# A two-layer decoder trunk: pairs by seven products, transposes in eights, a normalization finished after the product, and a table of places

## The chip, the cores and the metric

The kernel runs on one core of a Trainium2 chip. The metric is the device time of one execution in microseconds (us). Three runs of the kernel before took 1648.97, 1651.66 and 1651.95 us; their median is 1651.66 us.

## The reference

Tokens: 512 rows of 1024 features. The trunk has two layers, each with a half-weighted SwiGLU feed-forward (FFN), a token mixer and a second FFN; layer 0 mixes with a gated linear recurrence (RG-LRU), layer 1 with a causal spatial gate over chunks of 128 positions. So there are four FFNs, called f1 to f4 here, in the order f1, recurrence, f2, f3, spatial gate, f4.

```python
def rms_norm(x, g):
    y = xf * lax.rsqrt(jnp.mean(xf * xf, axis=-1, keepdims=True) + NORM_EPS)
    return y * g
def swiglu(x, w_in, w_out):                     # w_in 1024 x 5632, w_out 2816 x 1024
    g, u = jnp.split(x @ w_in, 2, axis=-1)
    return (jax.nn.silu(g) * u) @ w_out
def recurrent_mixer(x, ...):                    # w_in 1024 x 2048
    y, r = jnp.split(x @ w_in, 2, axis=-1)
    r = causal_depthwise_conv(r, conv_w, conv_b)
    h = rg_lru(r, ...)                          # two block-diagonal gates, then a scan over the rows
    return (jax.nn.gelu(y) * h) @ w_out
h = x
for i in range(2):
    h = h + 0.5 * swiglu(rms_norm(h, ffn1_norm[i]), ...)
    h = h + mixer(rms_norm(h, mix_norm[i]), ...)
    h = h + 0.5 * swiglu(rms_norm(h, ffn2_norm[i]), ...)
return rms_norm(h, final_norm)
```

## The kernel before, in words

**Arithmetic.** Every operand of a matrix product is cut into a rounded part ("hi") and the rest ("lo"); a product is three matmuls, hi by hi, lo by hi, hi by lo. The hi part is an ACT copy (L96), the lo part a DVE subtraction (L87); `split` does it for activations, `Sub.split` for a weight block of 128 x 1024 numbers (tiles `raw`, `whi`, `wlo`).

**Seven products.** `seven` computes a 2 x 2 block product with seven products instead of eight: P1, P2, P5, P6, P3, P7, Q4, each in one or more cuts of the inner dimension. P1, P6, P7 and Q4 gather in the PSUM banks A, P2 in B, P5 and P3 in C; in the output products Q4 has its own bank Q. The left sides are blocks of the activations (A11, A12, A22; the names give token half and feature half) and sums of them (S1 from A21, S2, S4, S3, in that order). The right sides are sums of weight blocks, made by DVE additions or by adding DMAs from POOL. After its last cut a product is read out (`p1` to `q4`): products that share a bank must not start before the readout of the one ahead.

**FFN.** An FFN has 22 column tiles of 128: in three parts, a pair of two tiles and a chunk of four, then twice two chunks of four. `chunk` uses `seven`; `pair_plain` (L695) computes the two tiles with eight products of 512 columns, gate and value side by side, and is the first work of each FFN. After each part `out_blocks` multiplies with `w_out` and adds to the residual `X`. Between them the hidden blocks are transposed on PE (128 x 128 each, tile `e`), four blocks after one product and four after the next, into a pool of two PSUM banks (`aux`).

**Norms.** RMSNorm's factor is applied after the product, by row, except ahead of the recurrence: there the product comes out with the rows along the free axis, so `TileNorm` (L490) scales the rows of `X` first (tile `xn`), transposes them (`xt`, L516) and cuts them into `zh`, `zl`; the first 256 rows are done when the first half of the residual is done, the other 256 when the last product (Q4) of f1 is.

**Order.** The program is a list `subs` of product cuts. The loop at the end goes through it: at step `i` it runs the actions hooked to the phases "pre" and "mid", with the weight splits up to three steps ahead (`SPLIT_AHEAD`) between them, then "rest", the loads, the matmuls of step `i`, then "end" and "late". Engines run their own instructions strictly in this order of issue, so the place of an action says what it stands behind on its engine. The places are written at each call of `hook`. Loads are issued by SP, adding DMAs by POOL.

Of the kernel before, what the change touches and what calls it, by code (L numbers as in the profile page):

```python
# [11 lines left out]
ALU = mybir.AluOpType  # L12
# [17 lines left out]
FF_PARTS = (("p", 4), (4, 4), (4, 4))  # L30
# [6 lines left out]
KORDER = (0, 2, 4, 6, 1, 3, 5, 7)  # L37
# [15 lines left out]
def trunk(ctx: ExitStack, tc: tile.TileContext, a: dict, out: bass.AP):  # L53
# [158 lines left out]

    def run(phase):
        for fn in hooks.pop((now[0], phase), []):
            fn()
# [17 lines left out]
    class S:  # L233
        z = None
        rt = None

# [4 lines left out]
    class Group:  # L241
# [12 lines left out]
        def turn(self, src, where=None):  # L254

            ps = (where or aux)("e")[:, : self.n * H]
            for q in range(self.n):
                for s in range(2):
                    o = q * H + s * P
                    nc.tensor.transpose(ps[:, o : o + P], src(q, s), ident)  # L260
            return ps
# [19 lines left out]
        def stage(self, n, name, src, gains=None, parts=True, where=None):  # L281

            st = {}
            hook(n, "end", lambda: st.update(ps=self.turn(src, where)))
            first = name == "A21"
            hook(n + 1, "pre" if first else "mid", lambda: self.take(name, st.pop("ps"), gains))
            if parts:
                hook(n + 1, "mid", lambda: self.parts("S1" if first else name))

        def both(self, n, name, src, then, then_src):  # L290

            st = {}

            def take():
                self.take(name, st.pop(name))
                self.take(then, st.pop(then))
                for b in (name, then):
                    if b != "A22":
                        self.parts("S1" if b == "A21" else b)

            hook(n, "end", lambda: st.update({name: self.turn(src), then: self.turn(then_src)}))
            hook(n + 1, "mid", take)
# [29 lines left out]
    def seven(block, cuts, left, w, posts, order=None, own=False, apart=False, joined=None):  # L332
# [6 lines left out]
        bk, raw, held = {}, {}, []  # L339
# [4 lines left out]
        def mm_of(prod, ci):  # L344
# [5 lines left out]
            def mm(sub):  # L350
# [6 lines left out]
                for s in range(2):  # L357
                    ps = bk[name, s]
# [10 lines left out]
                    if closes and prod in posts:  # L369
                        posts[prod](s, ps)  # L370
            return mm

        for prod, ci in order:
# [5 lines left out]
            if prod == "P1":  # L379
                r = raw[11, ci] = new(0, 0)  # L380
            elif prod == "P2":
                r = new(1, 0)
            elif prod == "P5":
                if own:
                    raw[11, ci] = new(0, 0, (0, 1))
                    if joined:
                        then = block(1, 1, cuts[ci])
                else:
# [3 lines left out]
            elif prod == "P6" and joined:  # L392
                r, then = raw[11, ci], block(1, 0, cuts[ci])
# [5 lines left out]
            elif prod == "P7":  # L399
                r = new(0, 1, (1, 1)) if own else raw[12, ci]  # L400
            else:
                r = raw[11, ci]
# [6 lines left out]

    def square(t, n):  # L410
        junk = slot(name="junk")
        act(junk, xt(t, n), AF.Square, accum_out=ss[:, n * TT + t : n * TT + t + 1])

    class Root:
# [7 lines left out]
        def root(self):  # L422
            act(self.s, self.v, AF.Sqrt)

        def get(self, r):
            q = tiny(self.w)
# [6 lines left out]
    def rstd(n, *phases, cols=slice(0, TT), new=True):  # L433
# [3 lines left out]
        def mean():  # L437
            st["r"] = Root((ss[:, :TT][:, cols], ss[:, TT:][:, cols]), cols.stop - cols.start)

        def newton():  # L440
            if new:
                S.rt = cp.tile([P, TT], F32, tag="rt", name=nm("rt"))
            st["r"].get(S.rt[:, cols])

        for (d, phase), fn in zip(phases, (mean, lambda: st["r"].root(), newton)):
            hook(n + d, phase, fn)
# [3 lines left out]
    def squares(n, phase, name):  # L450
        t0, c = QUARTER[name]
        hook(n, phase, lambda: (square(t0, c), square(t0 + 1, c)))

    class BlockNorm:


        def __init__(self, grow, block=False):
            self.g = [Group(2), Group(2)]
            self.grow, self.block = grow, block
# [5 lines left out]

        def quarter(self, name):
            n = now[0]
            squares(n + 1, "mid", name)
# [953 lines left out]
```

## Time and profile before

| | us |
|---|---|
| median of three runs | 1651.66 |
| the profiled execution | 1650.1 |
| its span on the core | 1648.3 |
| PE busy in the span | 1619.0 (98%) |
| DVE busy | 1379.7 (84%) |
| ACT busy | 1043.5 (63%) |
| POOL busy | 220.2 (13%) |

The profiled execution is 1.6 us under the median, and its span 1.8 us under its own time. PE's busy time counts from the start of a matmul to its modelled end, and matmuls overlap: what a matmul costs in a stream is the distance from start to start, not its duration. The mean granted clock of PE is 0.996 of full speed over the span.

### The profile page before, as it was taken

Reading aid. Unit: us, or ns where it says so; the run is one execution under the profiler, and the core shown is the slowest. Engines: PE = TensorE matmul, PEld = TensorE weight load, DVE = VectorE, ACT = ScalarE, POOL = GpSimd, SP = SyncE. Lnnn points to the kernel's source line nnn. Section 1 sums busy time; section 2 is a strip of 40 time slices with the busy share of each in tenths; the row PEclk is TensorE's granted clock in tenths of the full one; section 3 lists DMA queues with packets and bytes.
Section 4 is the critical chain, followed back from the end, with each engine's and each line's share of the span. In section 5 each row is a group of like instructions: output and inputs, shape, how many; then the busy total and the mean of one; then the engine's idle time right before and its main releaser. Section 6 shows DMA issues by size and latency. Waiting matters only on the chain. (4 is left out here: it accounts for less than half of the span.)

```text
span 1648.3 us, 20809 instructions
## 1 busy us (share of the span) xinstructions
PE 1619.0 (98%) x7451; PEld 1330.3 (81%) x7451; DVE 1379.7 (84%) x1824; ACT 1043.5 (63%) x1502; POOL 220.2 (13%) x199
## 2 busy tenths in 40 slices
PE   8999999989999999999999999999999999999997
PEld 6788888878878888888888888888887788888885
DVE  5998897877798897887988977878978988879777
ACT  6656656666857656556676565566885766565655
POOL 1111111100010111111102111111211011121120
PEclk9999999999999999999999999999999999999999
DMA  6767876952363876876838768768887557686693
GB/s 206 166 174 171 205 170 151 217 139 77 102 152 91 185 174 161 216 182 156 204 97 181 172 163 208 180 159 204 219 193 182 145 123 191 166 205 165 158 232 83
DMA packets 163463, 277.20 MB, mean 168 GB/s; under 512 B 11440, under 2 KB 37664, under 8 KB 163360
## 3 DMA queue, kind: packets, MB, share of 16 engines
q1 hardware_dynamic: 114400, 183.79, 35.9%
q0 software_dynamic: 47168, 90.25, 32.6%
q10 hardware_dynamic: 1792, 1.84, 0.4%
q8 instruction: 58, 0.95, 0.2%
q14 instruction: 45, 0.37, 0.1%
HBM read 273.74 MB, written 2.10 MB: 167 GB/s over the span
## 5 line engine op out<-in xcount | busy, mean ns | idle before, releaser
L96 ACT ACTIVATE whi<-raw 128x1024 fp32r<-128x1024 f32 (+1 forms) x545 | 562.4, 1034 | 412.2 <-PE A L367 112.6
L87 DVE TENSOR_TENSOR wlo<-raw,whi 128x1024 fp32r<-128x1024 f32 (+1 forms) x545 | 646.7, 1189 | 192.9 <-ACT whi L96 191.9
L366 PE MATMUL A<-whi,hi 128*128 128x512 f32 x1016 | 405.5, 399 | 3.3 <-DVE x L93 3.3
L367 PE MATMUL A<-whi,lo 128*128 128x512 f32 x1016 | 398.4, 392 | 3.2 <-DVE lo L87 3.1
L368 PE MATMUL A<-wlo,hi 128*128 128x512 f32 x1016 | 398.2, 392 | 0.3 <-DVE wlo L87 0.3
L367 PEld LDWEIGHTS A<-whi,lo 128*128 128x128 f32 x1016 | 191.7, 189 | 43.6 <-DVE lo L87 5.7
L368 PEld LDWEIGHTS A<-wlo,hi 128*128 128x128 f32 x1016 | 191.7, 189 | 41.9 <-DVE wlo L87 0.7
L366 PEld LDWEIGHTS A<-whi,hi 128*128 128x128 f32 x1016 | 191.8, 189 | 41.3 <-issue 3.7
L367 PE MATMUL C<-whi,lo 128*128 128x512 f32 x560 | 218.6, 390 | 1.2 <-DVE lo L87 1.0
L366 PE MATMUL C<-whi,hi 128*128 128x512 f32 x560 | 218.5, 390 | 0.0
L368 PE MATMUL C<-wlo,hi 128*128 128x512 f32 x560 | 218.0, 389 | 0.0
L136 POOL DMA_DIRECT2D raw<-in_ffn_w_in_dram x80 | 96.4, 1205 | 755.7 <-DVE raw L87 588.8
L87 DVE TENSOR_TENSOR raw<-raw,raw 128x1024 f32<-128x1024 f32 (+1 forms) x118 | 141.4, 1199 | 0.5
L136 POOL DMA_DIRECT2D raw<-in_ffn_w_out_dram x74 | 85.5, 1162 | 379.3 <-DVE wlo L87 145.9
L87 DVE TENSOR_TENSOR lo<-a,hi 128x512 fp32r<-128x512 f32 (+1 forms) x194 | 125.9, 657 | 10.5 <-ACT hi L96 10.1
L367 PEld LDWEIGHTS C<-whi,lo 128*128 128x128 f32 x560 | 105.1, 188 | 25.4 <-DVE lo L87 3.8
L366 PEld LDWEIGHTS C<-whi,hi 128*128 128x128 f32 x560 | 105.1, 188 | 22.1 <-ACT c L96 0.3
L368 PEld LDWEIGHTS C<-wlo,hi 128*128 128x128 f32 x560 | 105.1, 188 | 21.6
L96 ACT ACTIVATE hi<-a 128x512 fp32r<-128x512 f32 (+1 forms) x194 | 115.9, 600 | 4.6 <-DVE a L87 2.4
L96 ACT ACTIVATE c<-A 128x512 f32<-128x512 f32 x132 | 77.6, 595 | 59.1 <-PE A L368 58.6
L366 PE MATMUL B<-whi,hi 128*128 128x512 f32 x280 | 112.2, 401 | 0.0
L368 PE MATMUL B<-wlo,hi 128*128 128x512 f32 x280 | 109.3, 390 | 0.0
(160 smaller groups left out, 2093.8 us busy)
## 6 DMA issues: line engine op xcount, KB each, us to landing
raw<-in_ffn_w_in_dram SPq DMA_DIRECT2D x160, 512.0 KB, 4.4
raw<-in_ffn_w_out_dram SPq DMA_DIRECT2D x100, 512.0 KB, 5.3
raw<-in_ffn_w_in_dram POOLq DMA_DIRECT2D x80, 512.0 KB, 7.6
raw<-in_ffn_w_out_dram POOLq DMA_DIRECT2D x62, 512.0 KB, 8.3
raw<-in_sg_w_in_dram SPq DMA_DIRECT2D x20, 512.0 KB, 6.2
raw<-in_rec_w_in_dram SPq DMA_DIRECT2D x16, 512.0 KB, 3.9
raw<-in_ffn_w_in_dram SPq DMA_DIRECT2D x30, 256.0 KB, 4.0
raw<-in_sg_w_in_dram POOLq DMA_DIRECT2D x12, 512.0 KB, 8.5
```

The lines of the kernel that those rows point to most:

```text
L87: nc.vector.tensor_tensor(out=o, in0=x, in1=y, op=op)
L96: nc.scalar.activation(out=o, in_=x, func=f, **k)
L136: nc.gpsimd.dma_start(out=self.v, in_=src, accum_op=ALU.add)
L366: nc.tensor.matmul(ps, zh, wh, start=begin, stop=False, **k)
L367: nc.tensor.matmul(ps, zl, wh, start=False, stop=False, **k)
L368: nc.tensor.matmul(ps, zh, wl, start=False, stop=end, **k)
```

## The change

Six things change at once.

- **Pairs by seven products.** In f2, f3 and f4 the pair of column tiles goes through `chunk` and `seven` too, with 256 columns per product and all four inner blocks in one cut. f1 keeps `pair_plain`, in the middle of its first chunk (`between`). The chunk of four comes first in every FFN.
- **Transposes in eights.** The blocks of two products (A11 and A12, or A22 and A21) are transposed together, in `both` and `BlockNorm.turn`; a transposing bank comes from `aux` or from the matmul pool, by the table.
- **New opening.** f1 starts with P1 and P2 of the chunk. The loads alternate between a quarter of a row block of `x` and a weight block.
- **Last product's order.** f4's last output goes P1, P2, P6, P5, P7, Q4, P3 instead of P1, P5, P2, P6, P7, Q4, P3, with the weight sums rearranged to fit.
- **Half-wide norm.** `RecNorm` scales and transposes only the first 256 rows ahead of the recurrence's products. The other 256 are transposed unscaled, and their factor, laid along the free axis by two transposes (`rtw`), multiplies the right half of each of the sixteen product banks on DVE (`wide`).
- **The table.** `PLAN` has 916 entries: 201 weight splits one or two steps ahead instead of three, 121 banks for transposes, and the places of readouts and other actions; `soon` looks a place up, and readouts of `seven` may be put off.

```diff
+LATER_PARTS = ((4, 2), (4, 4), (4, 4))
+
+PLAN = {
+    "L0": 1, "L1": 2, "L10": 2, "L101": 1, "L104": 2, "L110": 2, "L111": 1, "L112": 2, "L114": 1, "L115": 1,
...
+    "f1c0postP3": (0, "late"), "f1c0postP5": (0, "end"), "f1c0s3": (4, "end"),
...
-KORDER = (0, 2, 4, 6, 1, 3, 5, 7)
+KORDER = (4, 5, 6, 7, 0, 1, 2, 3)
...
+    def soon(key, d, phase, fn, n=None):
+        d, phase = PLAN.get(key, (d, phase))
+        hook((now[0] if n is None else n) + d, phase, fn)
+
+    def home(key):
+        return bank if PLAN.get(key + "@") else aux
...
                     if closes and prod in posts:
-                        posts[prod](s, ps)
+                        when = PLAN.get(f"{key}post{prod}")
+                        if when is None:
+                            posts[prod](s, ps)
+                        else:
+                            late.add((name, s))
+                            hook(now[0] + when[0], when[1],
+                                 lambda s=s, ps=ps: (posts[prod](s, ps), late.remove((name, s))))
...
             if prod == "P1":
                 r = raw[11, ci] = new(0, 0)
+                if joined:
+                    then = block(0, 1, cuts[ci])
...
             elif prod == "P6" and joined:
-                r, then = raw[11, ci], block(1, 0, cuts[ci])
+                tile = raw[12, ci] = new(0, 1, (1, 1))
+                r, then = new(0, 0), block(1, 0, cuts[ci])
+                raw[6, ci] = r
...
+        def wide(self):
+            ps = self.ps["rt"] = aux("rt")
+            for t in range(2):
+                nc.tensor.transpose(ps[:, t * P : (t + 1) * P], S.rt[:, 2 + t : 3 + t].to_broadcast([P, P]), ident)
...
+            elif name == "A22":
+                soon("rnt1", 1, "end", lambda: self.turn("A22", self.plain))
+                soon("rnk1", 2, "mid", lambda: self.take("A22"))
...
-        ORDER = [(p, ci) for p in ("P1", "P5", "P2", "P6", "P7", "Q4", "P3") for ci in range(2)]
+        ORDER = [(p, ci) for p in ("P1", "P2", "P6", "P5", "P7", "Q4", "P3") for ci in range(2)]
...
+        def wide(ps):
+            tt(ps[:, H:], ps[:, H:], S.wide, ALU.mult)
...
     raws[0].halves = True
-    load_x(0, 512, 256)
-    load_x(0, 768, 256)
-    load_more(2)
-    load_x(0, 0)
+    for n, c in enumerate((0, 256, 512, 768)):
+        load_x(0, c, 256)
+        load_more(n + 1)
     load_x(2, 512)
+    load_more(5)
     load_x(2, 0)
     load_more()
...
-        upto = ahead.get(i, i + SPLIT_AHEAD)
-        for q in range(i, min(upto + 1, len(subs))):
-            if i >= 2 and q == upto and q + 1 < len(subs):
-                subs[q + 1].add()
-            subs[q].split()
+        for q in range(i, min(i + SPLIT_AHEAD + 1, len(subs))):
+            if q - PLAN.get(f"L{q}", SPLIT_AHEAD) <= i:
+                subs[q].split()
+            elif i >= 2:
+                subs[q].add()
```

Three places show how the order moves. First, PE in f4's last output, at the end of P6. Before, P7 follows at once in the same bank A:

```order
L368 MATMUL A_14065<-wlo_14154,hi_14183 128x512
L366 MATMUL A_14065<-whi_14153,hi_14183 128x512
L367 MATMUL A_14065<-whi_14153,lo_14184 128x512
L368 MATMUL A_14065<-wlo_14154,hi_14183 128x512
L366 MATMUL A_14064<-whi_14179,hi_14205 128x512
L367 MATMUL A_14064<-whi_14179,lo_14206 128x512
L368 MATMUL A_14064<-wlo_14180,hi_14205 128x512
L366 MATMUL A_14064<-whi_14179,hi_14205 128x512
```

Now P5 stands behind P6:

```order
L554 MATMUL A_14344<-whi_14391,hi_14443 128x512
L555 MATMUL A_14344<-whi_14391,lo_14444 128x512
L556 MATMUL A_14344<-wlo_14392,hi_14443 128x512
L554 MATMUL C_14496<-whi_14421,hi_14077 128x512
L555 MATMUL C_14496<-whi_14421,lo_14078 128x512
L556 MATMUL C_14496<-wlo_14422,hi_14077 128x512
```

The 24 matmuls of P5, in bank C, now lie between P6 and P7.

Second, PE at the start of the recurrence, after two half products of 24 matmuls (`r`). Before, the transposes of the other 256 rows read `xn`, which holds scaled rows:

```order
L218 MATMUL r_3262<-zh_3168,whi_3136 128x256
L219 MATMUL r_3262<-zl_3169,whi_3136 128x256
L220 MATMUL r_3262<-zh_3168,wlo_3137 128x256
L516 MATMUL xt_3287<-ident,xn_3223 128x128
L516 MATMUL xt_3287<-ident,xn_3227 128x128
```

Now, after one half product, they read `x` itself:

```order
L411 MATMUL r_3205<-zh_3179,whi_3083 128x256
L412 MATMUL r_3205<-zl_3180,whi_3083 128x256
L413 MATMUL r_3205<-zh_3179,wlo_3084 128x256
L730 MATMUL xt_3230<-ident,x 128x128 x4
L730 MATMUL xt_3235<-ident,x 128x128 x4
L411 MATMUL r_3256<-zh_3151,whi_3111 128x256
L412 MATMUL r_3256<-zl_3152,whi_3111 128x256
```

These eight need the third quarter of `X` (A22) alone; eight more follow one half product later.

Third, ACT in the recurrence, after the first five squares of the decay (`a<-g`). Before, a weight split, the last two gates (`g`, a table of their own) and a tanh stand ahead of the square roots (`tl<-tl`) on which the scans wait:

```order
L96 ACTIVATE a_811_3849<-g_3673 128x512
L96 ACTIVATE whi_3853<-raw_3410 128x1024
L96 ACT_TABLE_LOAD
L96 ACTIVATE g_3859<-gate_3824,vec 128x512
L96 ACTIVATE g_3861<-gate_3828,vec 128x512
L96 ACTIVATE tl_3863<-g_3859,lru_c 128x512
L96 ACT_TABLE_LOAD
L96 ACTIVATE tl_3496<-tl_3496 128x512
```

Now the square roots come first:

```order
L280 ACTIVATE a_807_3854<-g_3669 128x512
L280 ACT_TABLE_LOAD
L280 ACTIVATE tl_3489<-tl_3489 128x512
L280 ACTIVATE tl_3555<-tl_3555 128x512
L280 ACTIVATE tl_3608<-tl_3608 128x512
L280 ACTIVATE tl_3673<-tl_3673 128x512
L280 ACTIVATE tl_3714<-tl_3714 128x512
L280 ACTIVATE whi_3903<-raw_3457 128x1024
L280 ACTIVATE whi_3907<-raw_3459 128x1024
L280 ACT_TABLE_LOAD
L280 ACTIVATE g_3911<-gate_3832,vec 128x512
L280 ACTIVATE g_3913<-gate_3836,vec 128x512
```

The square roots have moved ahead of the last gates, and two weight splits have moved behind them.

514 lines of the change are left out of this document (297 added, 217 removed), and 175 rows, old and new, of the table PLAN.

## The prediction

> **What bounds the kernel now.** I read the page first, then a table of stages (busy time of each engine in stretches of the span), then PE's waits by releaser, and last the timeline at the places which these name.
>
> ```profile
> span 1648.3 us, 20809 instructions
> PE 1619.0 (98%) x7451; PEld 1330.3 (81%) x7451; DVE 1379.7 (84%) x1824; ACT 1043.5 (63%) x1502; POOL 220.2 (13%) x199
> ```
>
> PE is busy 98% of the span, so time can come from two sources only: less PE work, or less of PE's idle time. The stages show where that idle time is (start:end, length, then busy time and instructions by engine, the granted clock, DMA share and rate):
>
> ```profile
> core 0: us, PE busy (x) PEld busy (x) DVE busy (x) ACT busy (x) POOL busy (x), PEclk, DMA share, GB/s
> 0.00:40.00 40.00, 34.44 (x150) 24.98 (x150) 22.67 (x38) 26.18 (x49) 5.33 (x15) 1.00 0.64 212
> 40.00:110.00 70.00, 67.38 (x300) 53.73 (x301) 65.66 (x100) 45.26 (x69) 11.16 (x10) 1.00 0.76 174
> 320.00:353.00 33.00, 31.22 (x141) 24.41 (x139) 29.13 (x46) 21.48 (x37) 2.41 (x2) 1.00 0.66 154
> 353.00:367.00 14.00, 10.60 (x69) 9.93 (x69) 11.00 (x26) 9.52 (x22) 0.00 (x0) 0.88 0.28 81
> 367.00:460.00 93.00, 93.00 (x477) 79.70 (x476) 70.76 (x96) 69.18 (x100) 3.61 (x3) 1.00 0.33 94
> 460.00:480.00 20.00, 17.83 (x72) 14.33 (x71) 20.00 (x31) 9.77 (x13) 2.41 (x2) 0.91 0.56 120
> 480.00:1236.00 756.00, 755.40 (x3461) 622.26 (x3460) 642.27 (x802) 488.59 (x701) 107.52 (x91) 1.00 0.73 175
> 1236.00:1300.00 64.00, 61.48 (x310) 49.78 (x309) 55.73 (x92) 40.29 (x64) 7.25 (x6) 1.00 0.71 181
> 1600.00:1630.00 30.00, 26.68 (x113) 21.51 (x112) 24.19 (x33) 16.65 (x25) 3.61 (x3) 0.94 0.53 91
> ```
>
> Length less PE busy: 8.2 us in the first 110, 5.2 around the norm ahead of the recurrence (320 to 367), 2.2 at its end, 2.5 in the spatial mixer, 3.3 before the last products, and 0.6 in the 756 us of f2, f3 and their surroundings. Three of these stages have a lowered clock as well. At 0.88, 0.91 and 0.94 over 14, 20 and 30 us, 1.7 to 1.8 us go in each.
>
> ```profile
> PE A L366 <- DVE x L93: 3.3, 1, 3.3
> PE A L367 <- DVE lo L87: 3.1, 3, 2.2
> PE xt L516 <- ACT xn L96: 2.7, 3, 2.1
> PE e L260 <- DVE c L93: 2.1, 3, 1.0
> PE e L260 <- DMA x<-in_x_dram: 1.9, 2, 1.5
> PE warm L1308 <- DVE warm L1303: 1.3, 1, 1.3
> ```
>
> So the waits are few and long, each with an address: a readout in the last output, left sides after the scans, scaled rows ahead of the recurrence, hidden blocks, and `x` at the start. The clock follows the long ones:
>
> ```profile
> 462.79 0.80 PE L367 MATMUL A<-whi,lo 128*128 128x512 f32 x1 [2.17 <-DVE lo L87]
> 463.80 0.63 PE L366 MATMUL A<-whi,hi 128*128 128x512 f32 x1
> 464.23 0.63 PE L367 MATMUL A<-whi,lo 128*128 128x512 f32 x1
> 12.26 1.06 PE L260 MATMUL e<-ident,x 128*128 128x128 f32 x8 [1.54 <-DMA x<-in_x_dram]
> ```
>
> After 2.17 us of idle time the matmuls start 0.43 us apart; the idle 1.54 us of the opening lies in a stage at clock 1.00. "TensorE: Matmul & The Clock Gate" of the Trainium skill (section "Why this matters for your kernels") allows gaps up to about 3 us; here 2.17 us were enough, and the trace decides.
>
> **The change part by part.** *Pairs (f2, f3, f4).* What a matmul costs in a stream is the distance between starts. At 512 columns the rows below lie 26 matmuls apart, at 256 columns (the recurrence, both kinds of row) 17 and 18:
>
> ```profile
> 24.04 0.39 PE L717 MATMUL p<-whi,lo 128*128 128x512 f32 x1
> 29.93 0.39 PE L716 MATMUL p<-whi,hi 128*128 128x512 f32 x1
> 358.01 0.28 PE L219 MATMUL r<-zl,whi 128*128 128x256 f32 x1
> 360.05 0.28 PE L218 MATMUL r<-zh,whi 128*128 128x256 f32 x1
> 354.80 0.28 PE L218 MATMUL r<-zh,whi 128*128 128x256 f32 x1
> 357.15 0.28 PE L218 MATMUL r<-zh,whi 128*128 128x256 f32 x1
> ```
>
> That is 5.89 / 26 = 0.2265 us, then 2.04 / 17 = 0.120 and 2.35 / 18 = 0.131 us; half of 0.2265 would be 0.113. A pair took 8 products of 12 matmuls of 512: 96 x 0.2265 = 21.7 us. Now it is 7 products of 24 matmuls of 256: 168 x 0.120 = 20.2 us. Three pairs: **-4.8 us**, from -8.2 (0.113) to +0.6 (0.131). I take 0.120, the steady stretch; the slower one falls where DVE was cutting the same operands. By the Trainium skill, "TensorE: Matmul & The Clock Gate" (section "Back-to-back issue gap"), 256 columns would take 256 / 2.4 + 2.5 = 109 ns and the term would be an estimated -10.3 us, while its last section advises dimensions of at least 512; the rows show a price between, and they decide.
>
> On the other engines a pair costs one split more, and ten readouts of 256 columns instead of four:
>
> ```profile
> L96 ACT ACTIVATE whi<-raw 128x1024 fp32r<-128x1024 f32 (+1 forms) x545 | 562.4, 1034 | 412.2 <-PE A L367 112.6
> L87 DVE TENSOR_TENSOR wlo<-raw,whi 128x1024 fp32r<-128x1024 f32 (+1 forms) x545 | 646.7, 1189 | 192.9 <-ACT whi L96 191.9
> L87 DVE TENSOR_TENSOR s<-e,a 128x256 f32<-128x256 f32 x4 | 1.7, 413 | 0.0
> ```
>
> On DVE that is 1.2 + 6 x 0.41 = 3.7 us per pair. I cost it at nothing, because DVE is idle 114 us of the 756 between 480 and 1236; without that cover it would be 11 us for the three.
>
> *Last output.* PE waits 3.3 us for P6's readout from bank A before P7 may start, and a slow clock adds 1.8. In the new order 24 matmuls of P5, 24 x 0.2265 = 5.4 us, stand between them, more than wait and readout together. P3 is late next, if anything, and has P7 and Q4 ahead of it (10.9 us). **-5.1 us** (0 to -5.1).
>
> *Norm ahead of the recurrence.* 320 to 367 loses 5.2 idle and 1.7 in the clock. The second set of transposes waited for rows that need Q4's readout, squares, root and scaling. Now they need readouts alone, and Q4's has two half products, 2 x 24 x 0.120 = 5.8 us, and eight transposes as cover; the factor is needed only when the right half of the first bank is complete. The first set moves between the halves of Q4, which gives its rows 2.7 us more but its cutting 2.7 us less ahead of the first half product. I take **-6.0** of 6.9; the other bound, if the cutting is late by 1 us more than now, is +1. The price is sixteen multiplications on DVE at 0.41 = 6.6 us, and two transposes. DVE has 22 us free between 367 and 460.
>
> *End of the recurrence.* 2.2 idle and 1.8 in the clock. There the scans and not the products are late:
>
> ```profile
> 426.99 1.28 ACT L96 ACT_TABLE_LOAD   x1
> 431.47 2.71 ACT L96 ACTIVATE tl<-tl 128x512 f32<-128x512 f32 x5
> 432.13 0.69 DVE L87 TENSOR_TENSOR pr<-pr,tl 128x512 f32<-128x512 f32 x1 [2.71 <-ACT tl L96]
> ```
>
> From 432.13 on DVE works without a pause and the first left side lands at 462.8. With the square roots moved ahead of gates and a split, the table load follows at 426.99 - 1.03 = 425.96 and the first root at about 427.3 instead of 431.5; a multiplication ahead takes back 0.4, so the scans start 3.8 us sooner. By the order, one more weight split (1.2) and five multiplications (2.1) stand between first scan and left side, so it lands 0.5 us sooner. That leaves 1.7 us of idle time, between the 1.54 that left the clock alone and the 2.17 that did not. **-2.0 us**, from -4.0 (wait gone) to +3.3 (the head start is not used).
>
> *Opening and f1's first part.* 8.2 us idle, of which 1.3 (`warm`) stay. The waits for `x` go if each quarter comes with its weight block. Against it: by PE's order three transposed quarters, not two, now stand ahead of the first product, so 1.83 MB must land instead of 1.05; at 212 GB/s that is up to 3.7 us. Then 48 matmuls (10.9 us) run on data that have landed. I take **-4.0**, from -6.9 to +2.5.
>
> *Spatial mixer.* 2.5 us idle; its small products are spread out in eights between larger ones, which leaves DVE time for each: **-2.0** (-2.5 to 0). The single waits of the 756 us: **-0.3**.
>
> *Transposes in eights.* Their number stays (616 and 618 matmuls of 128 columns in the two programs); the runs fall from 144 to 84. A run of four and of eight, up to the second matmul behind it:
>
> ```profile
> 628.90 0.60 PE L260 MATMUL e<-ident,c 128*128 128x128 f32 x4
> 629.57 0.39 PE L367 MATMUL A<-whi,lo 128*128 128x512 f32 x1
> ...
> 1252.34 1.03 PE L260 MATMUL e<-ident,c 128*128 128x128 f32 x8
> 1253.44 0.40 PE L367 MATMUL A<-whi,lo 128*128 128x512 f32 x1
> ```
>
> Two fours take 2 x 0.67 - 0.23 = 1.11 us for the same matmuls, an eight 1.10: 60 x 0.01 = **-0.6** (0 to -1).
>
> *New waits.* The table moves 201 splits from three steps ahead to two or one, on ACT and DVE. Behind a split that waits for a free buffer stands all of ACT's other work (the 412 us of idle time ahead of `whi`, 112.6 of them waiting for PE), so this frees readouts. But a split takes 1.03 + 1.19 = 2.2 us and a step of 12 matmuls 2.7: one DVE instruction of 1.2 us ahead makes a split that is one step ahead 0.7 late, and PE waits for it. 76 are one step ahead. I allow three: **+2**, from 0 to +12.
>
> The sum: -4.8 - 5.1 - 6.0 - 2.0 - 4.0 - 2.0 - 0.3 - 0.6 + 2 = -22.8. From the profiled execution, 1650.1, that is a span of 1625.5 and a time of 1627.3; the median of the runs lies 1.6 above the profiled one, so I predict **1628.9 us**.
>
> **Rivals.** *Narrow matmuls bring nothing*: at 0.131 the pairs cost +0.6 instead of -4.8, so 1634. For it speaks that this distance stands in the trace and that DVE will be busier there; against it the longer steady stretch. The skill's advice on 512 columns is this rival.
>
> *Nearly all idle time goes*: every wait above except the warm-up is filled. Pairs -4.8, the stages -5.1 - 6.9 - 4.0 - 6.9 - 2.5 - 0.6, transposes -0.6: 1651.7 - 31.4 = 1620. For it: the waits are few and each gets work put in front. Against: DVE stays at 84% and more.
>
> *Splits too close* (slower than before): if more than 33 of the 76 splits that are one step ahead are 0.7 us late, the 22.8 + 2 us are eaten; with 60 late the time is 1651.7 - 24.8 + 42 = 1669. For it: DVE already waits 191.9 us for `whi`, so splits arrive barely ahead. Against: PE's waits for `wlo` are almost nothing now, and ACT has 37% free.
>
> *The table takes back what the rest gives*: some 33 such waits, no change.
>
> **How the numbers follow.** Forecast 0.61 (own range 1621 to 1639), nearly all idle time 0.20, narrow matmuls 0.12, splits too close 0.05, no change 0.02. For eight in ten, the range goes from 1612 (all low bounds, -35, give 1617; 5 more if PE also loses less around its short waits than I can price) to 1641 (new waits at +12 instead of +2 give 1639, and 2 more from the opening). A measurement of this kernel can tell about 0.2%, 3.3 us, from no change. Faster 0.93, within 0.02, slower 0.05.
>
> **What would show it.** Right: PE without a wait before P7 of the last output, and no lowered clock there nor at the start of the recurrence; matmuls of 256 columns in f2 to f4 at 0.12 us; the left side after the scans still late by one to two us. Wrong: waits of PE for `wlo` or `whi` spread through f2 to f4, a first product later than 10 us, waits for a free bank ahead of transposes, or DVE without idle time in the pairs.

## The result

| | before | after |
|---|---|---|
| median of four runs, us | 1650.32 (1647.36 to 1651.95) | 1621.63 (1619.54 to 1622.18) |
| ratio after to before | | 0.9826, 95% interval 0.9808 to 0.9844 |
| profiled execution, us | 1650.1 | 1621.8 |
| its span, us | 1648.3 | 1620.1 |

The change takes 28.7 us off; 22.8 were forecast, and 1621.6 lies inside the forecast's own range (1621 to 1639), at its lower end. The forecast time, 1628.9, is 7.3 off; 1.3 of that is the base, since the fourth run of the kernel before brought its median from 1651.66 to 1650.32. The result is nearer to the rival "nearly all idle time goes" (1620) than to the forecast.

The page of the changed kernel: its span, its busy times and the group of weight cutting on ACT (busy time, mean ns of one, then the idle time ahead of it and what ended most of it):

```profile
span 1620.1 us, 21202 instructions
PE 1603.2 (99%) x7669; PEld 1338.8 (83%) x7669; DVE 1394.1 (86%) x1860; ACT 1040.4 (64%) x1535; POOL 225.0 (14%) x203
L280 ACT ACTIVATE whi<-raw 128x1024 fp32r<-128x1024 f32 (+1 forms) x551 | 556.4, 1027 | 337.2 <-DVE raw L271 132.1
```

PE runs 218 instructions more (3 x 72 in the pairs, two transposes), is busy 15.8 us less, and its idle time in the span fell from 29.3 to 16.9 us. The idle time of ACT ahead of `whi` fell from 412.2 to 337.2 us: the cutting of weights holds it up less than before.

The same stages as before, at the places where they now lie (start:end, length, then busy time and instructions by engine, granted clock, DMA share and rate):

```profile
0.00:40.00 40.00, 37.11 (x156) 28.37 (x157) 24.95 (x33) 28.74 (x55) 6.33 (x16) 1.00 0.68 232
40.00:110.00 70.00, 70.00 (x319) 57.20 (x319) 67.31 (x113) 45.86 (x72) 10.20 (x10) 1.00 0.71 169
...
345.00:367.00 22.00, 19.97 (x164) 19.25 (x162) 14.82 (x31) 10.60 (x25) 0.00 (x0) 1.00 0.19 55
367.00:452.00 85.00, 84.06 (x385) 70.11 (x385) 72.57 (x104) 66.52 (x94) 2.61 (x3) 0.98 0.35 98
452.00:472.00 20.00, 17.88 (x75) 13.76 (x76) 20.00 (x31) 11.54 (x16) 3.40 (x3) 1.00 0.52 113
472.00:1216.00 744.00, 743.75 (x3583) 624.06 (x3584) 643.37 (x811) 480.96 (x713) 111.95 (x95) 1.00 0.75 181
1216.00:1279.00 63.00, 63.00 (x327) 53.15 (x326) 58.88 (x95) 43.45 (x67) 7.27 (x7) 1.00 0.75 183
1573.00:1603.00 30.00, 30.00 (x138) 24.91 (x137) 30.00 (x42) 20.95 (x31) 3.07 (x3) 1.00 0.53 111
```

The first 110 us lose 2.9 us of idle time (8.2 before), the spatial mixer none (2.5), the end of f4 none (3.3), f2 and f3 0.25 (0.6). The recurrence is the exception: 345 to 367 still loses 2.0, and 452 to 472 still 2.1. The low clock at the end of f4 and after the scans is gone; one after 367 is new. The waits of PE say the same by releaser:

```profile
PE e L454 <- DMA x<-in_x_dram: 1.6, 2, 0.9
PE gate L411 <- ACT hi L280: 1.6, 1, 1.6
PE A L555 <- DVE lo L271: 1.3, 1, 1.3
PE A L556 <- DVE wlo L271: 1.2, 3, 0.6
PE r L411 <- DVE zl L277: 1.0, 1, 1.0
PE C L556 <- DVE wlo L271: 0.8, 1, 0.8
...
```

Two more of 0.2 us each, for `lo` ahead of a gate and for `wlo` in bank B, and 1.3 us for the first warm-up matmul as before, and that is all that the list shows: 9.2 us. The five waits for `wlo` (2.2 us together) are new, and so is the one ahead of the gates.

For the bookkeeping, stages are better cut at one and the same product in both traces, since PE's busy time hides short gaps. Lengths in us between the starts of named matmuls:

| from | to | before | after | difference |
|---|---|---|---|---|
| start of the span | f1, first part, `Q` | 107.52 | 102.12 | -5.4 |
| that | f1, last `Q` | 238.84 | 235.92 | -2.9 |
| that | recurrence, output, `Q` | 152.91 | 151.63 | -1.3 |
| that | f2, last `Q` | 332.52 | 329.64 | -2.9 |
| that | f3, last `Q` | 332.82 | 329.31 | -3.5 |
| that | spatial mixer, `Q` | 135.13 | 130.06 | -5.1 |
| that | f4, last `Q` | 330.42 | 322.97 | -7.5 |
| that | end of the span | 18.13 | 18.46 | +0.3 |

Sixteen transposes (1.7 us) moved across the border after f1's last `Q`, so the second and third rows belong together: -4.2 us for the rest of f1, the norm and the recurrence, where -8.0 was forecast for the norm and the scans alone. The spatial mixer brought 3.1 more than forecast.

Three places in PE's timeline. First the pairs, then the gates and the first left side after the scans:

```profile
536.64 0.28 PE L554 MATMUL A<-whi,hi 128*128 128x256 f32 x1
539.51 0.28 PE L554 MATMUL B<-whi,hi 128*128 128x256 f32 x1
...
367.57 0.50 PE L411 MATMUL gate<-hi,hi 128*128 128x512 f32 x1 [1.60 <-ACT hi L280]
368.89 0.63 PE L411 MATMUL gate<-hi,hi 128*128 128x512 f32 x1
369.32 0.63 PE L412 MATMUL gate<-lo,hi 128*128 128x512 f32 x1
...
453.82 0.49 PE L555 MATMUL A<-whi,lo 128*128 128x512 f32 x1 [1.35 <-DVE lo L271]
```

The first two rows are 24 matmuls apart: 2.87 / 24 = 0.1196 us, the price taken for 256 columns. After the gates' wait of 1.60 us, 512 columns cost 0.43 us instead of 0.2265; from about 372.2 on the distances are back at 0.12 for 256. The left side after the scans is late by 1.35 us, and here the clock stays up.

### The profile page after: what moved, and what is told of

It is laid out like the page before. It is cut to its first block, busy times and chain, and to the rows that moved or that the text cites. A ratio compares the mean times of both kernels' runs of the same rounds, so it can differ in the third digit from the quotient of the medians.

```text
span 1620.1 us, 21202 instructions
## 1 busy us (share of the span) xinstructions
PE 1603.2 (99%) x7669; PEld 1338.8 (83%) x7669; DVE 1394.1 (86%) x1860; ACT 1040.4 (64%) x1535; POOL 225.0 (14%) x203
## 4 chain that ended last, share of the span: by engine, by line
PE 90%; DVE 5%; ACT 2%; DMA 1%; issue 1%; POOL 0%; SPq 0%; ACTq 0%; DVEq 0%
PE A L556 14%; PE A L554 14%; PE A L555 14%; PE C L555 8%; PE C L556 8%; PE C L554 8%; PE B L554 4%; PE B L556 4%; PE B L555 4%; PE e L454 3%; PE Q L555 1%; PE Q L554 1%; PE Q L556 1%; DVE wlo L271 1%; PE r L411 1%; PE r L413 1%
## 5 line engine op out<-in xcount | busy, mean ns | idle before, releaser
L280 ACT ACTIVATE whi<-raw 128x1024 fp32r<-128x1024 f32 (+1 forms) x551 | 556.4, 1027 | 337.2 <-DVE raw L271 132.1
L554 PE MATMUL A<-whi,hi 128*128 128x512 f32 (+1 forms) x1112 | 428.8, 386 | 0.1
L556 PE MATMUL A<-wlo,hi 128*128 128x512 f32 (+1 forms) x1112 | 424.5, 382 | 1.2 <-DVE wlo L271 1.2
L555 PE MATMUL A<-whi,lo 128*128 128x512 f32 (+1 forms) x1112 | 423.9, 381 | 1.5 <-DVE lo L271 1.3
L556 PE MATMUL C<-wlo,hi 128*128 128x512 f32 (+1 forms) x608 | 231.7, 381 | 0.8 <-DVE wlo L271 0.8
L555 PE MATMUL C<-whi,lo 128*128 128x512 f32 (+1 forms) x608 | 232.0, 382 | 0.0
L554 PE MATMUL C<-whi,hi 128*128 128x512 f32 (+1 forms) x608 | 232.1, 382 | 0.0
L271 DVE TENSOR_TENSOR raw<-raw,raw 128x1024 f32<-128x1024 f32 x120 | 143.7, 1201 | 0.3
L280 ACT ACTIVATE c<-A 128x512 f32<-128x512 f32 (+1 forms) x150 | 83.1, 568 | 69.9 <-PE A L556 69.4
L554 PE MATMUL B<-whi,hi 128*128 128x512 f32 (+1 forms) x304 | 116.5, 383 | 0.0
L556 PE MATMUL B<-wlo,hi 128*128 128x512 f32 (+1 forms) x304 | 115.9, 381 | 0.2 <-DVE wlo L271 0.2
```

Source lines behind the costliest of these rows:

```text
L271: nc.vector.tensor_tensor(out=o, in0=x, in1=y, op=op)
L280: nc.scalar.activation(out=o, in_=x, func=f, **k)
L554: nc.tensor.matmul(ps, zh, wh, start=begin, stop=False, **k)
L555: nc.tensor.matmul(ps, zl, wh, start=False, stop=False, **k)
L556: nc.tensor.matmul(ps, zh, wl, start=False, stop=end, **k)
```

## The experiments

All times are medians, in us. The change is at 1621.6, the kernel before at 1649.9 beside these runs.

### The last output's order

```diff
-        ORDER = [(p, ci) for p in ("P1", "P2", "P6", "P5", "P7", "Q4", "P3") for ci in range(2)]
+        ORDER = [(p, ci) for p in ("P1", "P2", "P5", "P6", "P7", "Q4", "P3") for ci in range(2)]
...
-    "f4o2postP6": (2, "pre"),
```

> P5 goes back ahead of P6 in the last output, P7 right behind P6, and P6's readout is issued at once; everything else as in the change. Forecast's theory: PE waits about 3.3 us for the readout ahead of P7 and starts again at the lower clock (1.7 to 1.8 us): +5.1 us against the changed kernel's 1621.6, so about 1626.7. Rival (the readout is early enough by itself, now that its place on DVE is chosen by the table): no wait, 1621.6.

Measured: 1629.7 (1629.1 to 1630.3), +8.1. PE's timeline there, ahead of P5's second half and of P7:

```profile
1589.79 0.50 PE L555 MATMUL C<-whi,lo 128*128 128x512 f32 x1 [1.68 <-DVE lo L271]
...
1601.69 0.47 PE L554 MATMUL A<-whi,hi 128*128 128x512 f32 x1 [3.64 <-ACT hi L280]
...
1603.73 0.63 PE L555 MATMUL A<-whi,lo 128*128 128x512 f32 x1
1604.16 0.63 PE L556 MATMUL A<-wlo,hi 128*128 128x512 f32 x1
```

DVE at the same time:

```profile
1598.60 2.35 DVE L271 TENSOR_TENSOR wlo<-raw,whi 128x1024 fp32r<-128x1024 f32 x2
1600.87 1.27 DVE L277 SCALAR_TENSOR_TENSOR x<-A,x 128x512 f32<-128x512 f32 x2
```

And ACT:

```profile
1600.50 1.13 ACT L280 ACTIVATE hi<-a 128x512 fp32r<-128x512 f32 x2
```

The wait ahead of P7 is back with 3.64 us, and the lower clock follows (0.43 us between matmuls). P7 starts at 1601.69, and two things end just ahead of it: the first of the two readouts from bank A (`x<-A,x`), behind two weight cuts on DVE, at about 1601.5, and the left sides on ACT (`hi`), which the trace names, at about 1601.6. So the size of the term is confirmed, 3.6 + 1.7 for the clock = 5.3 with 5.1 forecast; that the readout alone makes the wait is not shown by this run (in the kernel before, the trace names the readout). Another 1.68 us are P5's left side, which in this order is due 5.4 us sooner. The last 1.1 of the 8.1 us were not traced; the places in the table were made for the new order.

### The pairs

```diff
-                    chunk(f"{key}c{f0}", w_in, f0, n, groups[-1])
+                    if n == 2:
+                        pair_plain(f"{key}p", w_in, f0, groups[-1])
+                    else:
+                        chunk(f"{key}c{f0}", w_in, f0, n, groups[-1])
```

> The pairs of f2, f3 and f4 again by eight products of 512 columns (96 matmuls of 0.2265 us) instead of seven of 256 (168 of 0.120 us), at the same place; the table's other entries keep their meaning. Forecast's theory: +1.6 us a pair, +4.8 us, about 1626.4. Rival 1, narrow matmuls bring nothing: -0.6 us, 1621.0. Rival 2, a narrow matmul takes half of a wide one: +8.2 us, 1629.8.

(The splits behind a pair keep the distances of their products.) Measured: 1633.4 (1631.2 to 1634.9), +11.8, above all three expectations. From `Q` to `Q` f2 takes 333.30 us (329.64 in the change), f3 333.47 (329.31), f4 326.96 (322.97): 3.7, 4.2 and 4.0 more, together 11.8. The matmuls, at 0.2265 and 0.120 us, are 1.6 of each. Of the other 7.0 us, the list of PE's waits shows 5.1:

```profile
PE A L554 <- ACT hi L280: 3.9, 4, 1.3
PE A L555 <- DVE lo L271: 1.8, 3, 1.4
PE C L556 <- DVE wlo L271: 1.5, 2, 0.8
```

The change has no wait of the first kind, and 1.3 and 0.8 of the others. So -4.8 for the matmuls stands: from f2's first pair matmul to the first `A` matmul behind the pair, with eight transposes in it, it is 22.66 us here (536.66 to 559.32) and in the change 21.01 to the transposes behind it (536.64 to 557.65), 1.65 us a pair. The time of the run doesn't measure it alone. A reason for the rest, argued and not tested: eight plain products at this place deliver their results to a table that was made for seven.

### How early weights are cut

```diff
-            if q - PLAN.get(f"L{q}", SPLIT_AHEAD) <= i:
+            if q - (PLAN.get(f"L{q}", SPLIT_AHEAD) if i < 12 else SPLIT_AHEAD) <= i:
```

> From the twelfth step on every weight split is three steps ahead again, as in the kernel before; the table's places and banks stay. Forecast's theory: splits one or two steps ahead cost PE some three waits, so three ahead is 0 to 2 us faster: 1619.6 to 1621.6. Rival: splits three ahead stand in front of readouts on ACT and DVE that are now due, so short waits come back: 1 to 6 us slower, 1623 to 1628.

Measured: 1658.1 (1657.6 to 1660.2), +36.5, and 0.56% slower than the kernel before (ratio 1.0056, 1.0039 to 1.0072). Both expectations fell, the forecast's by its sign and the rival's by its size. PE's waits, and ACT's group of weight cuts:

```profile
PE A L555 <- DVE lo L271: 6.5, 8, 1.8
PE C L555 <- DVE lo L271: 4.8, 8, 1.0
PE e L454 <- DVE c L277: 4.2, 7, 1.6
PE A L554 <- ACT hi L280: 3.6, 3, 1.9
```

```profile
L280 ACT ACTIVATE whi<-raw 128x1024 fp32r<-128x1024 f32 (+1 forms) x551 | 562.3, 1028 | 449.8 <-DVE raw L271 198.0
```

PE waits for left sides (`hi`, `lo`) and for hidden blocks (`c`), hardly for weights. ACT stands idle 449.8 us ahead of weight cuts (337.2 in the change): a cut that is issued early waits for its raw block or its buffer, and everything behind it in ACT's order waits as well. The table's other places were made for short distances, so the 36.5 us are the price of long distances in this table, not of long distances as such. A smaller step was tried with the splits that the table sets one step ahead set two ahead, from the twelfth step on:

```diff
+            if q - (max(2, PLAN.get(f"L{q}", SPLIT_AHEAD)) if i >= 12 else PLAN.get(f"L{q}", SPLIT_AHEAD)) <= i:
```

> From the twelfth step on, splits that the table sets one step ahead are two steps ahead; the others stay as in the change. Forecast's theory (a split one step ahead is now and then 0.7 us late, three times in the sum): 0 to 2 us faster, 1619.6 to 1621.6. Rival (a split that comes sooner stands ahead of left sides and readouts on ACT and DVE; three steps ahead for all of them cost 36 us): 3 to 15 us slower, 1625 to 1637.

Measured: 1634.4 (1633.0 to 1635.7), +12.7: the rival. ACT's idle time ahead of weight cuts is 356.0 us here, and the waits are again for left sides and hidden blocks (5.4 us for `lo` in A and C where the change has 1.3, and 3.3 for `c`). The five waits for `wlo` of the change are gone, 2.2 us, as the forecast had it; only that is the small side of the matter.

### Most of the table left out

> Of the table's 916 entries 630 are left out: the split distances from the fifteenth step on, nearly all bank entries, and the places of the second and third parts of f1 to f4. Norms, opening, first chunks, recurrence, spatial mixer and the last outputs keep theirs. The split distances alone were worth 36 us in the changed kernel (1658.1 without them). Theory A (distances and places belong together: places chosen for short distances are wrong for long ones): without both it is better than without the distances alone, 1640 to 1652. Theory B (each brings its own): 1665 or more.

Measured: 1673.7 (1672.6 to 1676.1), +52.1, ratio to the kernel before 1.0146 (1.0132 to 1.016): theory B. Against the run with all splits three ahead it is another 15.6 us slower. Waits for left sides in bank A alone are 10.3 us for `lo` in 15 places and 5.7 for `hi`. The new opening, pairs, eights, last order and norm, with 630 of the 916 places at their defaults, are slower than the kernel before, whose places were written for its own order. Short distances with the other places at their defaults were not run, so what the distances bring by themselves stays open.

### The first product

```diff
-    "opt0A12": (0, "pre"),
```

> The transposes of the first half of the third quarter (A12) come behind the first product instead of ahead of it, one entry of the table. Theory: the first product waits for x that it does not need; it starts at about 8 us instead of 10.0, and x has landed when the transposes follow, so -2 us, about 1619.6. Rival: the wait for x only moves behind the first product, 0 us, or the idle time grows and the lower clock lasts longer, +1 us.

Measured: 1619.5 (1618.1 to 1620.1), -2.1. In the change the first product stands behind four transposes that wait for the third quarter of `x`:

```profile
9.28 1.08 PE L454 MATMUL e<-ident,x 128*128 128x128 f32 x4 [0.86 <-DMA x<-in_x_dram]
10.02 0.77 PE L554 MATMUL A<-whi,hi 128*128 128x512 f32 x1
```

With the entry left out it starts 2.1 us sooner, and the transposes behind it find `x` landed:

```profile
7.88 0.99 PE L554 MATMUL A<-whi,hi 128*128 128x512 f32 x1
...
12.24 0.60 PE L454 MATMUL e<-ident,x 128*128 128x128 f32 x4
```

How much of the 2.1 us is the entry's is less sure than the median looks. The two ranges overlap (the change: 1619.5 to 1622.2). And in the profiles f1's last `Q` comes 1.4 us sooner than in the change (336.65 to 338.04), but 0.4 later than in the run with the early left side (336.23), which has the change's opening. What differs there is when the matmuls reach their full rate: at about 10.8 us here, 13.6 in the change and 10.3 in that run (see the last section).

### The norm ahead of the recurrence

In the first of two kernels (with small helpers for it that the diff leaves out) the second 256 rows are scaled before they are transposed, as before, and the sixteen multiplications of the products fall away. In the second the transposes also come one half product sooner, where the kernel before had them.

```diff
-                soon("rnt1", 1, "end", lambda: self.turn("A22", self.plain))
-                soon("rnk1", 2, "mid", lambda: self.take("A22"))
...
+                hook(n + 1, "rest", lambda: self.rows(2))
+                hook(n + 2, "end", lambda: (self.turn("A22", self.normed), self.turn("A21", self.normed)))
+                hook(n + 3, "mid", lambda: (self.take("A22"), self.take("A21")))
...
-            tt(ps[:, H:], ps[:, H:], S.wide, ALU.mult)
```

> The norm ahead of the recurrence as in the kernel before for the second 256 rows: they are scaled first, and both their sets of transposes come after the last readout; the sixteen multiplications of the products are gone. The rest of the change stays. Forecast's theory: +6.0 us, about 1627.6. Rival (from the two traces: the stretch from the end of the first part of f1 to the last product behind the recurrence became only 4.2 us shorter, because a wait of 1.6 us for the first gates came in and the left side after the scans stays late, so what was won ahead of the recurrence was in part handed on): +1 to +4 us, 1622.6 to 1625.6, with the gates or the scans less late than in the changed kernel.

Measured: 1617.3 (1615.7 to 1618.0), 4.4 us *faster* than the change. All expectations had the other sign.

> As the run with scaled rows (1617.3), but the second set of transposes comes after two half products, where the kernel before had it, and not after three. Theory A (in that run one half product more ahead did the work, and the norm's new form has only the price of its sixteen multiplications on DVE): the wait ahead of the transposes comes back with 2.7 us and 0 to 1.7 us of lower clock, 1620 to 1621.6, about the time of the change. Theory B (the place does not matter, since readouts come early by the table): 1617.3.

Measured: 1622.7 (1620.5 to 1623.3), +1.0: theory A; from the change the ranges do not separate it. From f1's last `Q` to the `Q` behind the recurrence, in the change, after three half products and after two, one row of a table of stretches each:

```profile
338.04:489.67 151.63, 146.54 (x747) 123.92 (x746) 130.90 (x198) 107.15 (x169) 7.22 (x6) 0.99 0.42 111
```

```profile
337.54:485.66 148.12, 144.74 (x746) 122.55 (x745) 126.11 (x184) 108.16 (x170) 7.22 (x6) 1.00 0.43 113
```

```profile
336.52:490.16 153.64, 147.35 (x746) 125.22 (x744) 126.14 (x184) 108.20 (x170) 7.22 (x6) 0.98 0.42 110
```

After three half products scaled rows are no longer late, and the wait ahead of the transposes is almost nothing; after two it is 3.26 us, with the lower clock behind it:

```profile
355.15 2.25 PE L731 MATMUL xt<-ident,xn 128*128 128x128 f32 x16 [0.27 <-DVE xn L274]
```

```profile
354.12 3.86 PE L731 MATMUL xt<-ident,xn 128*128 128x128 f32 x16 [3.26 <-DVE xn L274]
```

So one half product more ahead (2.9 us of work) does what the norm's new form was forecast to do, and the new form has a price. DVE's group of multiplications in the change:

```profile
L271 DVE TENSOR_TENSOR r<-r,rtw 128x256 f32<-128x256 f32 x16 | 6.8, 425 | 4.0 <-PE r L413 4.0
```

DVE is busy 4.8 us more in the stretch (130.90 to 126.11), and each multiplication stands between a product and its readout. It is not hidden: without the multiplications the stretch is 3.5 us shorter (151.63 to 148.12). Some 0.7 of that is the lower clock behind the gates' wait, which only the change's execution has: the run with the first product earlier has the change's norm and no lower clock there, and takes 150.95. The other 2.8 are the price, the larger part behind the scans: from the first product there to `Q` it is 36.0 us instead of 37.7, where the left side is no longer late. It is 36.0 after two half products as well, so this part goes with the norm's form and not with the place of its transposes. For the remaining 1.1 us, ahead of the scans, form and place are not separated.

The same cure was put into the kernel before, with nothing of the change:

```diff
-                hook(n + 2, "end", self.turn)
-                hook(n + 3, "pre", lambda: self.take(1))
+                hook(n + 3, "end", self.turn)
+                hook(n + 4, "pre", lambda: self.take(1))
```

> The kernel before with one place moved: the second set of transposes ahead of the recurrence comes after three half products (24 matmuls of 256 columns each) instead of two, its cutting one step later too; nothing of the change is in it. Theory A (the stretch is bound by PE's order): the wait of 2.7 us ahead of these transposes and part of the lower clock go, -2.7 to -4.4 us, 1645.5 to 1647.2. Theory B (DVE's work up to the left side after the scans sets the end of the stretch): PE only comes earlier to that left side and waits there longer, 0 us, 1650.

Measured: 1645.6 (1644.3 to 1647.8), -4.3, ratio 0.9974 (0.9963 to 0.9984): theory A. Two numbers moved by one took as much as the stretch gained by the whole change (-4.2), in part because the lower clock behind these transposes (363.8 to 367.2 in the kernel before) is gone as well. The transposes start with no wait, and the left side after the scans is as late as before, not later:

```profile
363.35 1.91 PE L516 MATMUL xt<-ident,xn 128*128 128x128 f32 x16
...
458.71 0.50 PE L367 MATMUL A<-whi,lo 128*128 128x512 f32 x1 [2.17 <-DVE lo L87]
```

### The gates and the left side after the scans

Two entries of the table, each alone: the first gates one half product later, and the first left side cut as soon as its two products are there.

```diff
-    "r0gate": (2, "rest"),
```

> The first gate products come behind the half product that now follows them (24 matmuls of 256 columns, 2.9 us), one entry of the table. Theory A: PE's wait of 1.6 us for the gates' left side and the lower clock behind it (1.2 us) go: -2.8 us, 1618.8. Theory B: DVE works without a pause from 418 us to the left side at 452 us, and its start there does not depend on PE, so PE comes to the left side earlier and waits there longer: 0 us, 1621.6, or +1.7 if the longer wait lowers the clock.

Measured: 1621.3 (1621.2 to 1621.6), no change: theory B's time. The stretch is 151.07 us long instead of 151.63. The wait of 1.6 us ahead of the first gates is gone, but the second pair of gates now waits 1.3, a product waits 1.2 for a readout, the left side is late by the same 1.35 us, and the lower clock comes behind that.

```diff
+    "ypA110": (6, "late"),
```

> The first left side after the scans (A11) is cut right after its two products y*h, at the end of step 6, instead of together with A12 and S1 in step 7, one added entry of the table. Theory A: the wait of 1.35 us (1.6 from start to start) at the first product of the recurrence's output goes, and the next left side (A12) is in time behind its 2.7 us: -1.6 us, 1620.0. Theory B: DVE is busy without a pause there, so 0.7 us of cutting ahead makes A12 and S1 late by as much: 0 us, 1621.6.

Measured: 1620.1 (1619.4 to 1621.5), which the ranges don't separate from the change. The trace decides for theory B. The 1.35 us at the first product are gone, and the second product waits 0.51 + 0.81 = 1.32:

```profile
452.83 0.50 PE L554 MATMUL B<-whi,hi 128*128 128x512 f32 x1 [0.51 <-ACT hi L280]
454.15 0.50 PE L555 MATMUL B<-whi,lo 128*128 128x512 f32 x1 [0.81 <-DVE lo L271]
```

### What was won, in one kernel

Scaled rows after three half products, the third quarter's transposes behind the first product, the early left side, and a warm-up run of three matmuls instead of two.

> What was won in three runs, in one kernel: rows scaled ahead with the transposes after three half products (-4.4), the transposes of the third quarter behind the first product (-2.1), and the first left side after the scans cut early (-1.5); one more warm-up matmul of 512 columns fills 0.5 of the 0.8 us in which PE waits for x. Theory A (three places that do not meet): 1621.6 - 4.4 - 2.1 - 1.5 = 1613.6. Theory B (the run with scaled rows already has only 0.4 us of stall left at that left side): 1621.6 - 4.4 - 2.1 - 0.4 = 1614.7.

Measured: 1616.0 (1615.6 to 1616.2), ratio to the kernel before 0.9795 (0.9781 to 0.9808). It is the fastest kernel here, 5.7 us under the change, with no run in common between the two ranges; it is 1.3 to 2.4 us slower than the two expectations. The early left side adds nothing (148.20 us from `Q` to `Q` against 148.12 without it). Of the opening the trace shows f1's last `Q` 2.2 us sooner than in the run with scaled rows (335.38 to 337.54), but the medians differ by 1.3 only. A good part of those 2.2 us is again the start: matmuls 0.43 us apart go on until about 12.7 us there, and here only the first is slow (7.99).

## Why the prediction was right, and where it wasn't

**What bounds the kernel** was read rightly: PE's order, with a few long waits, each with an address. Every long wait named there outside the recurrence is gone, except that for `x` at the start (1.6 us, 1.9 before). Of the signs named for being right, one failed: the clock is still lowered at the start of the recurrence, from 368.8 to 372.2. Those named for being wrong stayed away: only two of the five waits for `wlo` lie in f2 to f4 (1.0 us together), no transpose waits for a bank, and DVE is busy 17.0 of the 21.0 us of f2's pair; the first product, at 10.02 us, sits on the bound of 10 us that was named. The rival "nearly all idle time goes" has the time and not the mechanism: it gave the norm and the recurrence 10.9 us, the table above shows 4.2, and PE still stands idle 16.9 us.

**Pairs, -4.8: right.** 0.1196 us at 256 columns, in f2, f3 and f4 alike; "narrow matmuls bring nothing" is out, and so is the lower bound of half a wide one. DVE took the added readouts without PE waiting for them.

**Last output, -5.1: right in size.** Undone it costs 3.6 us of waiting and 1.7 of clock. Which of readout and left side makes the wait in that run stays open, and the 1.7 do not follow every time (last section). P3 is not late, as said.

**Norm, -6.0: the term that failed.** Undone at its old place it is worth 1 us in the time, with ranges that overlap, and 2.0 in the stretch. Two steps of it were wrong. "DVE has 22 us free between 367 and 460" is an average over the stretch: the multiplications stand between products and their readouts, in a chain of multiplication, readout, convolution and gates, where DVE's free time elsewhere does not help; of the price, the 1.7 us behind the scans are measured, and this chain is the argued reason. And the wait had a cheaper cure that the working didn't look for: the distance of the transposes from the last readout, counted in half products. It also turned into a new wait, 1.6 us ahead of the first gates, with the lower clock behind it in the profiled execution; the forecast named none there.

**End of the recurrence, -2.0: its place right, its size not separable.** The left side was forecast to be late by 1.7 us, "between the 1.54 that left the clock alone and the 2.17 that did not", and is late by 1.35 with the clock up. The part from there to `Q` became 1.35 us shorter. The square roots alone were not tried, so how much of it is theirs stays open.

**Opening, -4.0: too small, and won elsewhere than said.** The first product is at 10.02 us, 3.0 later than before (up to 3.7 forecast), and the first part of f1 is over 5.4 sooner, 7.0 in the run with the early left side, where the clock came up sooner (`Q` at 100.48). The waits for `x`, which were to go, are still there and stand ahead of the first product now. What went is all idle time behind it: from the first product to `Q` PE was idle 6.3 us before and is idle 0.0 now. That the first product need not be so late, and that up to 2 us more were to be had, the forecast priced but didn't follow up.

**Spatial mixer, -2.0: too small by 3.1.** It was sized by idle time in a window of 64 us. From `Q` to `Q` the stage was 135.13 us long, and its matmuls at their distances (504 of 512 columns at 0.2265, 136 of 128 columns at 0.109) take 129.0: 6.1 us were there to be lost, because a gap inside a matmul's modelled duration counts as busy. In the change the same sum leaves 1.1. The same holds, smaller, for f2 and f3: 3.2 us beyond their pairs, where single waits and transposes were forecast at 0.9 for everything.

**New waits, +2: right as written, and beside the point.** The five waits for `wlo` are there, 2.2 us. But the step took the table to be a cost with a side benefit. With the table's other places as they are, it is the other way round: the same waits go when splits come two ahead, and 12.7 us are lost; three ahead, 36.5. "This frees readouts" stood in the forecast without a price. So "splits too close" and "the table takes back what the rest gives" are out, and the larger risk, that the other five edits with most of the table left out are slower than before (1673.7), was not among the rivals. That the sum came within 5.9 us owes something to luck, since errors cancel: by the table of stages 3.8 too much for f1, norm and recurrence, and 9.6 too little for the rest (1.4 in the opening, 3.1 in the spatial mixer, 5.1 in f2 to f4 with the new waits).

## What to carry to other kernels

When an engine waits for a chain, first count what stands between the chain's start and the wait, and try to put one more piece of independent work there: in the kernel before, two numbers moved by one brought 4.3 us, where new arithmetic on a busy engine brought about one. Work issued early on an in-order engine is not free; if its inputs or buffers are late, all that stands behind it is late too, so the earliest place and the best place differ. Size what a stage can give by its length less its instructions' distances, not by its idle time.

## What was not expected of the hardware

The same wait of 1.60 us ahead of the first gates was followed by the lower clock in some profiled executions and not in others. In the change (the rows above) matmuls then start 0.43 us apart; in the run with the first product earlier, behind the same wait, 0.23:

```profile
366.20 0.49 PE L411 MATMUL gate<-hi,hi 128*128 128x512 f32 x1 [1.60 <-ACT hi L280]
...
367.26 0.39 PE L413 MATMUL gate<-hi,lo 128*128 128x512 f32 x1
367.50 0.40 PE L411 MATMUL gate<-hi,hi 128*128 128x512 f32 x1
```

And more than twice that wait left the clock up once: ahead of P7, in the kernel before with its transposes after three half products, PE stands idle for 3.46 us, and the next matmuls start 0.23 us apart.

```profile
1618.85 0.47 PE L366 MATMUL A<-whi,hi 128*128 128x512 f32 x1 [3.46 <-DVE x L93]
1619.16 0.39 PE L367 MATMUL A<-whi,lo 128*128 128x512 f32 x1
1619.39 0.39 PE L368 MATMUL A<-wlo,hi 128*128 128x512 f32 x1
```

So a fixed threshold between 1.54 and 2.17 us, as the forecast used it, does not hold, and the 1.7 us of clock behind a long wait are not lost in every execution: something besides the length of the wait decides. The times of the low stretches point to when the gap falls. In the change the low clock lasted 3.41 us, a loss of 1.7, and more than half of the 3.41 us ahead of it were idle (PE busy for 1.59; the granted clock is the third number from the end):

```profile
365.43:368.84 3.41, 1.59 (x8) 1.01 (x7) 2.37 (x4) 0.85 (x2) 0.00 (x0) 1.00 0.00 0
368.84:372.25 3.41, 3.41 (x14) 3.07 (x13) 2.75 (x4) 2.85 (x4) 0.00 (x0) 0.50 0.00 0
```

The three low stretches of the kernel before also last 3.41 us each, from 363.77, 462.76 and 1623.29 on; they lie 98.99 and 1160.53 us apart, which is 29.0 and 340.0 times 3.413. So in that execution they begin on one grid of 3.413 us. The Trainium skill, "TensorE: Matmul & The Clock Gate" (section "What's actually happening"), says that the gate judges PE's activity in free-running windows of 3413 ns; the grid agrees with that. Which share of a window must be idle was not measured here.

The opening shows the same. With one and the same program order at the start, the full clock came only after 13.6 us in the change's profile and at about 10.3 in the run with the early left side, whose matmuls are 0.23 us apart from 10.45 on; its f1 ends 1.8 us sooner (`Q` at 336.23 against 338.04). A single profiled execution thus carries about 2 us of chance from the start, and effects of that size are better judged by stretches that begin later, or by medians of several runs. The column of granted clock does not show it: the first 40 us stand at 1.00 in the change.
